# Raw feed-forward weights in eight tiles of two chunks instead of four of four

## Chip, core and metric

The kernel runs on one core of one Trainium2 chip. The metric is the device time of one execution in microseconds (us); lower is better. TensorE is called PE in the profile, VectorE DVE, ScalarE ACT, GpSimd POOL and the queue of SyncE SP.

## The reference, cut to what matters

A decoder layer on 256 tokens of width 2048: a SwiGLU feed-forward, a mixer (sliding-window attention beside RWKV-7), cross-attention into a memory, and a second SwiGLU feed-forward. The change touches the two feed-forwards.

```python
D_MODEL, D_FF, SEQ = 2048, 5632, 256

def swiglu(h, w_gate, w_up, w_down):
    return (jax.nn.silu(h @ w_gate) * (h @ w_up)) @ w_down

x = x + 0.5 * swiglu(rms_norm(x, ffn1_norm[l]), ffn1_w_gate[l], ffn1_w_up[l], ffn1_w_down[l])
x = gated_parallel_mixer(x, ...)
x = memory_cross_attention(x, mem, ...)
x = x + 0.5 * swiglu(rms_norm(x, ffn2_norm[l]), ffn2_w_gate[l], ffn2_w_up[l], ffn2_w_down[l])
return rms_norm(x, final_norm)
```

All weights are float32 and are read once: 46 MB for each of the six feed-forward matrices.

## The kernel before

**Precision.** Each product is made of three matmuls in a rounded 32-bit format (fp32r): a value is split into a rounded part "hi" and a remainder "lo", and hi*hi, lo*hi and hi*lo are added (`times`, lines 485 to 487). ScalarE casts "hi" (line 409) and VectorE subtracts "lo" (line 410), both in `split_unit`. The buffers "hi" and "lo" are rings of three units.

**Units and items.** A *unit* is two chunks (KU = 2) of 128 rows by 512 columns of one weight matrix, 512 KB. An *item* is what one step of the product loop uses: one unit, or, where two column blocks are worked on together, a unit of each. Such pairs are gate with up, and two column blocks of down. The text calls the first of a pair gate and the second up. `weight_plan` lists all products; `units` and `items` are made from it once, in the order of use.

**Seven products in place of eight.** Of an item of a pair, 2 x 2 blocks are multiplied, and some items (SEVEN: pairs 0, 2, 3 and 4 of the eight in a gate/up block; others in down) do it in seven products (21 matmuls) in place of eight (24). For these POOL adds a chunk of the gate unit into the first chunk of the up unit while transferring it from DRAM (line 366, an accumulating DMA, table `added`). Then VectorE makes three sums (lines 438, 439, 440 in `divide`), and these are split into "thi" and "tlo" (lines 417, 418). In the second feed-forward pair 3 is *staged*: its sums are made during the mixer, kept in DRAM and loaded (`staged`, `first_sums`, `load_sums`).

**Where raw weights lie.** In the feed-forwards raw weights are loaded by SP into tiles "raw2" of four chunks (1 MB), of which there are four. One such tile holds two units of the same matrix: those of an even pair and of the odd pair behind it. So the units stand in the order gate (even), gate (odd), up (even), up (odd), and the two items are (0, 2) and (1, 3) of these. In the mixer and at the first units of the second feed-forward the tiles "raw" hold one unit each.

**What orders the work.** `next_item` asks for the loads of the eight units from the current item on, then divides the current item and the ones after it (AHEAD = 2 units). SP's queue is in order, and a load waits until its tile's last reader is done, mostly a "lo". VectorE's and ScalarE's queues are in order too, but their order isn't the written one: a scheduler places each instruction at build time, by when it believes its inputs to be there. `product_pair` multiplies; after each group of products `bg.tick()` lets background steps (transposes, norms, sums of the activations) put in their instructions. A gate/up *block* is 512 columns of gate and up over all 16 chunks, eight items; three groups of four, four and three blocks are each followed by their down products. The text calls blocks of a group first, middle and last.

Of the kernel before, what the change touches and what calls it, by code (L numbers as in the profile page):

```python
# [7 lines left out]
F32 = mybir.dt.float32  # L8
F32R = mybir.dt.float32r
AF = mybir.ActivationFunctionType  # L10
ALU = mybir.AluOpType
# [4 lines left out]
P = 128  # L16
# [11 lines left out]
KU = 2  # L28
# [6 lines left out]
AHEAD, LOADED = 2, 4  # L35
# [4 lines left out]
SEVEN_2, STAGED = (0, 2, 3, 4), (3,)  # L40
# [60 lines left out]
def weight_plan(a):  # L101

    w = {n: v[0] for n, v in a.items() if "_w_" in n or n.startswith("w_")}
    yield from feed_forward_plan(w["ffn1_w_gate"], w["ffn1_w_up"], w["ffn1_w_down"], False)
    yield None
    w_in = w["w_in"]
    cols = [0, 512, ATTN_W]
    for c in cols:  # L110
        yield w_in, 0, KD, c, 512
    yield w_in, 0, KD, C_RW + 3 * RW, 288
    for h in range(2):
        yield w_in, 0, KD, C_RW + RW + h * 512, 512
    for n in range(4):
        yield w_in, 0, KD, C_GATE + n * 512, 512
        yield w["w_proj_attn"], 0, 8, n * 512, 512
    for h in range(2):
        yield w_in, 0, KD, C_RW + h * 512, 512
        yield w_in, 0, KD, C_RW + 2 * RW + h * 512, 512  # L120
    for n in range(4):
        yield w_in, 0, KD, C_GATE + D + n * 512, 512
    for n in range(4):
        yield w["w_proj_rwkv"], 0, 8, n * 512, 512
    for n in range(4):
        yield w["w_out"], 0, KD, n * 512, 512
    yield w["w_cross_kv"], 0, KD, 0, 512
    yield w["w_cross_q"], 0, KD, 0, 512
    yield w["w_cross_kv"], 0, KD, 512, 512
    for n in range(4):  # L130
        yield w["w_cross_o"], 0, 4, n * 512, 512
    yield None
    yield from feed_forward_plan(w["ffn2_w_gate"], w["ffn2_w_up"], w["ffn2_w_down"], True)
# [3 lines left out]
def decoder_layer(ctx: ExitStack, tc: tile.TileContext, a: dict, out: bass.AP):  # L137
    nc = tc.nc
    act, dve, pool, pe = nc.scalar, nc.vector, nc.gpsimd, nc.tensor
# [126 lines left out]
    def flat(x):  # L266
        x = x[0]
        return x if len(x.shape) == 1 else x.rearrange("h d -> (h d)")
# [6 lines left out]
    first = fill()  # L275
# [5 lines left out]
    v = flat(a["rwkv_mu"])  # L281
# [7 lines left out]
    def late_vectors():  # L289
        while "pow" not in at:  # L290
            yield
        with tc.issue_after(at["pow"].ins):
            pool.dma_start(sinks[:], a["attn_sinks"].broadcast_to([P, 16]))
            fetch_gains()
            fetch_rv()
        yield from idle(12)
        fill_gains()
        fill_rv()
        dve.tensor_scalar(nk_k[:], k_k, -1.0, None, ALU.mult)
        dve.tensor_scalar(ok_a[:], k_a, -1.0, 1.0, ALU.mult, ALU.add)  # L300
# [11 lines left out]
    plan, units, items, ends, staged = [], [], [], [], {}  # L312
    for entry in weight_plan(a):
        if entry is None:
            ends.append(len(units))
            continue
        plan.append(entry)
        w, k0, nk, c0, n = entry
        if not isinstance(w, tuple):
            for k in range(k0, k0 + nk, KU):  # L320
                items.append(((len(units),), False))
                units.append((w, k, c0, n))
            continue
        for k in range(k0, k0 + nk, 2 * KU):
            u = len(units)
            units += [(v, k + i, c, 512) for v, c in zip(w, c0) for i in (0, KU)]
            for i in range(2):
                q = (k - k0) // KU + i
                if len(ends) == 2 and n == SEVEN_2 and q in STAGED:
                    staged[len(items)] = len(staged)  # L330
                items.append(((u + i, u + 2 + i), q in n))
    raws, parts, summed = {}, {}, {}
    first_sums = {items[i][0][1]: n for i, n in staged.items()}
    added = {which[1]: which[0] for i, (which, seven) in enumerate(items) if seven and i not in staged}
    sums_d = dram.tile([len(staged), P, 4, 512], F32, name="sums")
    at = {"item": 0, "product": 0, "pool": None}

    def load(u, pieces=None):

        if u >= len(units) or u in raws:  # L340
            return
        w, k, c0, n = units[u]
        wide = at["pool"] is not None and (u < ends[0] or u >= ends[1] + LOADED)
        m = 2 if wide else 1
        if wide:
            raw = at["pool"].tile([P, m * KU, n], F32, tag="raw2", name="raw2", bufs=4)
        else:
            raw = wp.tile([P, KU, n], F32, tag="raw", name="raw", bufs=4)
        for i in range(m):
            raws[u + i] = raw[:, i * KU : (i + 1) * KU, :]  # L350
        first = [v for v in (u, u + 1)[:m] if v in first_sums]
        for v in first:
            nc.sync.dma_start(raws[v][:, 0], sums_d[first_sums[v], :, 0, :])
        if first:
            pieces = ((slice(1, 4), nc.sync),)
            if first[0] > u:
                pieces = ((slice(0, 2), nc.sync), (slice(3, 4), nc.sync))
            elif len(first) == 2:
                pieces = ((slice(1, 2), nc.sync), (slice(3, 4), nc.sync))
        for i, queue in pieces or ((slice(0, m * KU), nc.sync),):  # L360
            rows = slice((k + i.start) * P, (k + i.stop) * P)
            queue.dma_start(raw[:, i], w[rows, c0 : c0 + n].rearrange("(a p) n -> p a n", p=P))
        for v in (u, u + 1)[:m]:
            if v in added:
                w, k, c0, n = units[added[v]]
                pool.dma_start(  # L366
                    raws[v][:, 0], w[k * P : k * P + P, c0 : c0 + n], accum_op=ALU.add,
                )

    def load_sums(i):  # L370

# [72 lines left out]
    def next_item():  # L444
        i = at["item"]
        at["item"] += 1
        u = items[i][0][0]
        for v in range(u, u + (2 * LOADED if at["pool"] is not None else LOADED)):
            load(v)
        divide(i)  # L450
        room = AHEAD
        for j in range(i + 1, min(i + 1 + AHEAD, len(items))):
            room -= len(items[j][0])
            if room < 0:
                break
            for v in items[j][0]:
                load(v)
            load_sums(j)
            divide(j)
        load_sums(i + 2)  # L460
        return parts[i]
# [337 lines left out]
    def blk(d, n):  # L799
        return d[:, n * 512 : (n + 1) * 512].rearrange("(t p) n -> p t n", p=P)  # L800

    W = {n: v[0] for n, v in a.items()}
# [7 lines left out]
    def aligned(sp):  # L810

        return sp.tile([P, 16], F32, name="shift")


    with tc.tile_pool(name="f1", bufs=1, reuse_waits="tile") as sp:
        aligned(sp)
        at["pool"] = sp
        x = sp.tile([P, 2, D], F32, name="x")

        def col(n):  # L820
            return x[:, :, n * 512 : (n + 1) * 512]

        n1 = Norm(g_ffn1)
        nc.sync.dma_start(col(0), blk(W["x"], 0))
        load(0, ((slice(0, 1), act), (slice(1, 2), nc.sync), (slice(2, 4), nc.sync)))
        nc.sync.dma_start(col(1), blk(W["x"], 1))
        load(2, ((slice(0, 2), nc.sync), (slice(2, 4), nc.sync)))
        for n in range(2, 4):
            nc.sync.dma_start(col(n), blk(W["x"], n))
            load(2 * n)  # L830
        for n in range(4):
            bg.spawn("feat", n1.block(n, col(n)))
        bg.spawn("const", late_vectors())
        hold = {}

        def done1(n):
            if n == 0:
                hold["n"] = Norm(g_mix)
            pool.dma_start(blk(x1d, n), col(n))
            bg.spawn("feat", hold["n"].block(n, col(n)))  # L840

        feed_forward(sp, x, n1, W["ffn1_w_gate"], W["ffn1_w_up"], W["ffn1_w_down"], done1)
        n2 = hold["n"]
        bg.drain()
        at["pool"] = None


    with tc.tile_pool(name="mx", bufs=1, reuse_waits="tile") as sp:
# [3 lines left out]
        def t4(name, shape=(P, 4, T), dt=F32):  # L852
            return sp.tile(list(shape), dt, tag="t4", name=name, bufs=N4)
# [651 lines left out]
        for n in range(4):  # L1505
            g, m = t4("gl", (P, 2, 512)), t4("ml", (P, 2, 512))
# [102 lines left out]
    with tc.tile_pool(name="f2", bufs=1, reuse_waits="tile") as sp:  # L1609
        room = aligned(sp)  # L1610
        at["pool"] = sp
        x = sp.tile([P, 2, D], F32, name="x")
# [92 lines left out]
```

## Time and profile before

| | before |
|---|---|
| median of 3 runs | 2391.59 us (2387.91 to 2400.15) |
| the profiled execution | 2391.23 us, span 2389.5 us |
| mean granted TensorE clock | 0.983 |
| PE busy | 2278.7 us (95%) |
| DVE busy | 1810.1 us (76%) |
| ACT busy | 1260.0 us (53%) |
| POOL busy | 213.7 us (9%) |
| moved by DMA | 487 MB, 204 GB/s on the mean |

Busy times are of one profiled execution. The span runs from its first to its last instruction. Idle time of an engine counts only where another engine waits for it; who waited for whom is read from semaphore events. A DMA's time is that from its issue to its landing, and the mean share is that of the 16 DMA engines.

### The profile page before, as it was taken

Reading aid. Unit: us, or ns where it says so; the run is one execution under the profiler, and the core shown is the slowest. Engines: PE = TensorE matmul, PEld = TensorE weight load, DVE = VectorE, ACT = ScalarE, POOL = GpSimd, SP = SyncE. Lnnn points to the kernel's source line nnn. Section 1 sums busy time; section 2 is a strip of 40 time slices with the busy share of each in tenths; the row PEclk is TensorE's granted clock in tenths of the full one; section 3 lists DMA queues with packets and bytes.
Section 4 is the critical chain, followed back from the end, with each engine's and each line's share of the span. In section 5 each row is a group of like instructions: output and inputs, shape, how many; then the busy total and the mean of one; then the engine's idle time right before and its main releaser. Section 6 shows DMA issues by size and latency. Waiting matters only on the chain.

```text
span 2389.5 us, 28663 instructions
## 1 busy us (share of the span) xinstructions
PE 2278.7 (95%) x10557; PEld 1839.0 (77%) x10557; DVE 1810.1 (76%) x2332; ACT 1260.0 (53%) x1649; POOL 213.7 (9%) x293
## 2 busy tenths in 40 slices
PE   9999998999999999999999999999999989998998
PEld 7677776777777877788888887887778767776776
DVE  6897787987888667877556666567788778877886
ACT  6465454554555557534444546465555455544554
POOL 1000000000000101110321030000000000000000
PEclk9999999999999999999999999999999999999999
DMA  7666666666666645676768685557666766666664
GB/s 253 189 212 193 192 206 188 205 201 192 209 200 195 187 128 151 194 229 208 213 217 266 205 283 184 184 192 248 211 203 208 222 194 221 203 189 207 208 220 146
DMA packets 244973, 487.04 MB, mean 204 GB/s; under 512 B 17163, under 2 KB 19440, under 8 KB 244832
## 3 DMA queue, kind: packets, MB, share of 16 engines
q1 hardware_dynamic: 221952, 433.62, 54.6%
q0 software_dynamic: 22416, 50.79, 10.5%
q8 instruction: 83, 1.36, 0.2%
q10 hardware_dynamic: 464, 0.79, 0.1%
q14 instruction: 58, 0.48, 0.1%
HBM read 461.47 MB, written 23.59 MB: 203 GB/s over the span
## 4 chain that ended last, share of the span: by engine, by line
PE 48%; DMA 23%; DVE 22%; issue 5%; ACT 2%; SPq 0%; POOLq 0%; POOL 0%; DVEq 0%; ACTq 0%
PE acc L485 11%; PE acc L486 11%; PE acc L487 11%; DVE lo L410 10%; DMA raw<-in_ffn_w_gate_dram 10%; DMA raw<-in_ffn_w_up_dram 7%; DMA raw<-in_ffn_w_down_dram 5%; DVE tlo L418 3%; PE mm L486 2%; PE mm L487 2%; PE mm L485 2%; PE tr L676 2%; DVE raw L439 2%; DVE raw L440 1%; ACT hi L409 1%
## 5 line engine op out<-in xcount | busy, mean ns | idle before, releaser
L409 ACT CAST hi<-raw 128x1024 fp32r<-128x1024 f32 (+1 forms) x770 | 801.6, 1045 | 786.4 <-PE acc L487 478.8
L410 DVE TENSOR_TENSOR lo<-raw,hi 128x1024 fp32r<-128x1024 f32 (+1 forms) x770 | 930.7, 1214 | 331.7 <-ACT hi L409 330.2
L485 PE MATMUL acc<-hi,xhi 128*128 128x512 f32 (+1 forms) x1136 | 450.6, 399 | 2.7 <-ACT xhi L703 2.3
L486 PE MATMUL acc<-lo,xhi 128*128 128x512 f32 (+1 forms) x1136 | 445.1, 392 | 2.7 <-DVE lo L410 2.7
L487 PE MATMUL acc<-hi,xlo 128*128 128x512 f32 (+1 forms) x1136 | 442.8, 390 | 0.0
L485 PEld LDWEIGHTS acc<-hi,xhi 128*128 128x128 f32 x1136 | 215.4, 190 | 50.6 <-issue 4.0
L486 PEld LDWEIGHTS acc<-lo,xhi 128*128 128x128 f32 x1136 | 214.6, 189 | 50.4 <-DVE lo L410 8.0
L487 PEld LDWEIGHTS acc<-hi,xlo 128*128 128x128 f32 x1136 | 214.3, 189 | 44.6 <-DVE xlo L704 1.0
L417 ACT CAST thi<-raw 128x1024 fp32r<-128x1024 f32 x212 | 168.3, 833 | 131.2 <-DVE raw L439 126.2
L418 DVE TENSOR_TENSOR tlo<-raw,thi 128x1024 fp32r<-128x1024 f32 x212 | 196.0, 950 | 2.2 <-ACT thi L417 1.9
L438 DVE TENSOR_TENSOR raw<-raw 128x512 f32<-128x512 f32 x96 | 66.1, 689 | 153.3 <-DMA raw<-in_ffn_w_gate_dram 112.1
L486 PE MATMUL mm<-lo,xhi 128*128 128x512 f32 x360 | 144.1, 400 | 31.2 <-DVE lo L410 31.2
L487 PE MATMUL acc<-hi,hlo 128*128 128x512 f32 x372 | 146.3, 393 | 0.0
L485 PE MATMUL acc<-hi,hhi 128*128 128x512 f32 x372 | 146.1, 393 | 0.1
L486 PE MATMUL acc<-lo,hhi 128*128 128x512 f32 x372 | 146.1, 393 | 0.0
L487 PE MATMUL mm<-hi,xlo 128*128 128x512 f32 x360 | 142.1, 395 | 0.0
L485 PE MATMUL mm<-hi,xhi 128*128 128x512 f32 x360 | 141.5, 393 | 0.0
L366 POOL DMA_DIRECT2D raw<-in_ffn_w_gate_dram x70 | 60.4, 904 | 882.2 <-DMA raw<-in_ffn_w_up_dram 342.4
L486 PEld LDWEIGHTS mm<-lo,xhi 128*128 128x128 f32 x360 | 68.5, 190 | 50.0 <-DVE lo L410 36.6
L486 PE MATMUL mm<-lo,chi 128*128 128x512 f32 x200 | 80.5, 402 | 5.6 <-DVE lo L410 5.6
L485 PE MATMUL mm<-hi,chi 128*128 128x512 f32 x200 | 80.7, 413 | 3.4 <-DVE u L638 1.8
L485 PEld LDWEIGHTS acc<-hi,hhi 128*128 128x128 f32 x372 | 70.4, 189 | 15.9 <-DVE x L649 1.7
(399 smaller groups left out, 3723.6 us busy)
## 6 DMA issues: line engine op xcount, KB each, us to landing
raw<-in_ffn_w_down_dram SPq DMA_DIRECT2D x88, 1024.0 KB, 6.2
raw<-in_ffn_w_gate_dram SPq DMA_DIRECT2D x84, 1024.0 KB, 5.7
raw<-in_ffn_w_up_dram SPq DMA_DIRECT2D x78, 1024.0 KB, 7.0
raw<-in_w_in_dram SPq DMA_DIRECT2D x136, 512.0 KB, 3.8
raw<-in_ffn_w_gate_dram POOLq DMA_DIRECT2D x70, 256.0 KB, 4.3
raw<-in_w_out_dram SPq DMA_DIRECT2D x32, 512.0 KB, 4.5
raw<-in_w_proj_attn_dram SPq DMA_DIRECT2D x16, 512.0 KB, 4.0
raw<-in_w_proj_rwkv_dram SPq DMA_DIRECT2D x16, 512.0 KB, 4.7
```

Of the source, the lines that this page charges most:

```text
L366: pool.dma_start(raws[v][:, 0], w[k * P : k * P + P, c0 : c0 + n], accum_op=ALU.add,)
L409: at["hi"] = act.copy(hi[:, s], raw[:, s])
L410: at["lo"] = dve.tensor_tensor(lo[:, s], raw[:, s], f32(hi[:, s]), ALU.subtract)
L417: act.copy(hi[:], v[:, :n])
L418: dve.tensor_tensor(lo[:], v[:, :n], f32(hi[:]), ALU.subtract)
L438: dve.tensor_tensor(t[0][:, 0], ru[:, 1], ru[:, 0], ALU.add)
L439: dve.tensor_tensor(t[0][:, 1], t[0][:, 0], rg[:, 0], ALU.subtract)
L440: dve.tensor_tensor(t[1][:, 0], t[0][:, 0], rg[:, 1], ALU.add)
L485: pe.matmul(o, xh, hi, start=first, stop=False, **how)
L486: pe.matmul(o, xh, lo, start=False, stop=False, **how)
L487: pe.matmul(o, xl, hi, start=False, stop=last, **how)
L676: pe.transpose(b[:, o : o + P], tok[:, t, col : col + P], ident[:])
```

## The change

Units of a pair now stand in the order of their use (gate, up, gate, up), every item is two neighbouring units, and each unit has a tile "raw2" of its own: two chunks, 512 KB, eight tiles. The memory is the same. A tile is loaded by one transfer of 512 KB (two of 256 KB for the staged sums) where one of 1 MB was, and the special cases for two units in one tile are gone. At the start the loads of the first eight units are issued one by one, between the same loads of x. In the built program SP issues 850 transfers where it issued 600; POOL's 208 are the same. The instructions of the mixer stand in the same order on each engine; those of the feed-forwards on VectorE, ScalarE and TensorE are the same in number and kind, but the scheduler has put many of them in another order. Lines move up by 12 (line 438 is 426 after, 410 is 398, 366 is 354).

```diff
-        for k in range(k0, k0 + nk, 2 * KU):
-            u = len(units)
-            units += [(v, k + i, c, 512) for v, c in zip(w, c0) for i in (0, KU)]
-            for i in range(2):
-                q = (k - k0) // KU + i
-                if len(ends) == 2 and n == SEVEN_2 and q in STAGED:
-                    staged[len(items)] = len(staged)
-                items.append(((u + i, u + 2 + i), q in n))
+        for k in range(k0, k0 + nk, KU):
+            q = (k - k0) // KU
+            if len(ends) == 2 and n == SEVEN_2 and q in STAGED:
+                staged[len(items)] = len(staged)
+            items.append(((len(units), len(units) + 1), q in n))
+            units += [(v, k, c, 512) for v, c in zip(w, c0)]
...
         w, k, c0, n = units[u]
-        wide = at["pool"] is not None and (u < ends[0] or u >= ends[1] + LOADED)
-        m = 2 if wide else 1
-        if wide:
-            raw = at["pool"].tile([P, m * KU, n], F32, tag="raw2", name="raw2", bufs=4)
+        if at["pool"] is not None and (u < ends[0] or u >= ends[1] + LOADED):
+            raw = at["pool"].tile([P, KU, n], F32, tag="raw2", name="raw2", bufs=8)
         else:
             raw = wp.tile([P, KU, n], F32, tag="raw", name="raw", bufs=4)
-        for i in range(m):
-            raws[u + i] = raw[:, i * KU : (i + 1) * KU, :]
-        first = [v for v in (u, u + 1)[:m] if v in first_sums]
...
-        for i, queue in pieces or ((slice(0, m * KU), nc.sync),):
+        raws[u] = raw
+        if u in first_sums:
+            nc.sync.dma_start(raw[:, 0], sums_d[first_sums[u], :, 0, :])
+            pieces = ((slice(1, 2), nc.sync),)
+        for i, queue in pieces or ((slice(0, KU), nc.sync),):
             rows = slice((k + i.start) * P, (k + i.stop) * P)
             queue.dma_start(raw[:, i], w[rows, c0 : c0 + n].rearrange("(a p) n -> p a n", p=P))
-        for v in (u, u + 1)[:m]:
-            if v in added:
-                w, k, c0, n = units[added[v]]
-                pool.dma_start(
-                    raws[v][:, 0], w[k * P : k * P + P, c0 : c0 + n], accum_op=ALU.add,
-                )
+        if u in added:
+            w, k, c0, n = units[added[u]]
+            pool.dma_start(
+                raw[:, 0], w[k * P : k * P + P, c0 : c0 + n], accum_op=ALU.add,
+            )
...
         nc.sync.dma_start(col(0), blk(W["x"], 0))
-        load(0, ((slice(0, 1), act), (slice(1, 2), nc.sync), (slice(2, 4), nc.sync)))
-        nc.sync.dma_start(col(1), blk(W["x"], 1))
-        load(2, ((slice(0, 2), nc.sync), (slice(2, 4), nc.sync)))
-        for n in range(2, 4):
+        load(0, ((slice(0, 1), act), (slice(1, 2), nc.sync)))
+        load(1)
+        for n in range(1, 4):
             nc.sync.dma_start(col(n), blk(W["x"], n))
             load(2 * n)
+            load(2 * n + 1)
```

More of the change, by code (lines that the diff above doesn't have):

```diff
@@ L342, in load @@
         w, k, c0, n = units[u]
-        wide = at["pool"] is not None and (u < ends[0] or u >= ends[1] + LOADED)
-        m = 2 if wide else 1
-        if wide:
-            raw = at["pool"].tile([P, m * KU, n], F32, tag="raw2", name="raw2", bufs=4)
+        if at["pool"] is not None and (u < ends[0] or u >= ends[1] + LOADED):
+            raw = at["pool"].tile([P, KU, n], F32, tag="raw2", name="raw2", bufs=8)
         else:
             raw = wp.tile([P, KU, n], F32, tag="raw", name="raw", bufs=4)
-        for i in range(m):
-            raws[u + i] = raw[:, i * KU : (i + 1) * KU, :]
-        first = [v for v in (u, u + 1)[:m] if v in first_sums]
[L352 to L359, printed above, removed]
-        for i, queue in pieces or ((slice(0, m * KU), nc.sync),):
+        raws[u] = raw
[3 more added lines that the diff above has]
+        for i, queue in pieces or ((slice(0, KU), nc.sync),):
             rows = slice((k + i.start) * P, (k + i.stop) * P)
             queue.dma_start(raw[:, i], w[rows, c0 : c0 + n].rearrange("(a p) n -> p a n", p=P))
-        for v in (u, u + 1)[:m]:
-            if v in added:
-                w, k, c0, n = units[added[v]]
-                pool.dma_start(
-                    raws[v][:, 0], w[k * P : k * P + P, c0 : c0 + n], accum_op=ALU.add,
-                )
+        if u in added:
[3 more added lines that the diff above has]
+            )
     def load_sums(i):
```

## The prediction

> **What bounds the kernel now.** I read the busy time by stretches first, then the waits, then the timeline of one stall. The stretches are the first feed-forward (to about 760 us), the mixer and the second feed-forward (from about 1625 us); columns are us, then each engine's busy us (instructions), the granted clock, DMA share and GB/s.
>
> ```profile
> span 2389.5 us, 28663 instructions
> 60.00:760.00 700.00, 655.35 (x2807) 521.14 (x2807) 587.13 (x723) 362.76 (x413) 46.57 (x54) 0.98 0.65 198
> 760.00:1625.00 865.00, 856.75 (x4461) 703.34 (x4459) 569.32 (x779) 461.32 (x716) 118.35 (x167) 1.00 0.66 205
> 1680.00:2389.50 709.50, 660.27 (x2828) 528.81 (x2827) 572.09 (x702) 368.37 (x422) 36.52 (x45) 0.97 0.64 203
> ```
>
> TensorE is at work 99% of the mixer and 93 to 94% of the feed-forwards: 45 us and 49 us stand idle there, and the change touches the feed-forwards alone. VectorE is at 84% and 81% there, near enough to TensorE that a pause of VectorE is felt. DMA moves the same 200 GB/s at the same share in all three, so it isn't bytes that are short. What pauses VectorE shows in the waits (total us, times, longest):
>
> ```profile
> DVE raw L438 <- DMA raw<-in_ffn_w_gate_dram: 112.1, 45, 6.6
> ACT hi L409 <- DMA raw<-in_ffn_w_gate_dram: 67.1, 17, 6.7
> PEld mm L486 <- DVE lo L410: 56.9, 26, 5.7
> PE mm L486 <- DVE lo L410: 46.4, 20, 5.3
> DVE raw L438 <- DMA raw<-in_ffn_w_down_dram: 41.1, 18, 5.6
> SPq L362 <- DVE lo L410: 562.0, 110, 14.1
> ```
>
> Line 438 is the first sum of a seven-product item. It reads the up tile after POOL's accumulating transfer (line 366) has added a gate chunk to it. VectorE stood 153 us before these sums (112.1 + 41.1, 63 of 96 times), and TensorE's largest waits are for the "lo" that stand behind them. The last row (asked for the first 760 us alone) is SP's: its loads wait for VectorE's "lo", since that releases a raw tile. So there is a loop: release, load, accumulation, sum, next release. One worst turn of it, on the timeline:
>
> ```profile
> 343.73 2.35 DVE L410 TENSOR_TENSOR lo<-raw,hi 128x1024 fp32r<-128x1024 f32 x2
> 345.00 0.37 SPq L362 DMA_DIRECT2D raw<-in_ffn_w_gate_dram  x1
> 346.10 0.37 SPq L362 DMA_DIRECT2D raw<-in_ffn_w_up_dram  x1
> ...
> 352.42 1.21 DVE L410 TENSOR_TENSOR lo<-raw,hi 128x1024 fp32r<-128x1024 f32 x1
> 353.55 0.68 DVE L439 TENSOR_TENSOR raw<-raw,raw 128x512 f32<-128x512 f32 x1
> 354.16 0.68 DVE L440 TENSOR_TENSOR raw<-raw,raw 128x512 f32<-128x512 f32 x1
> 354.76 1.21 DVE L410 TENSOR_TENSOR lo<-raw,hi 128x1024 fp32r<-128x1024 f32 x1
> 355.75 0.86 POOL L366 DMA_DIRECT2D raw<-in_ffn_w_gate_dram  x1 [12.86 <-DMA raw<-in_ffn_w_up_dram]
> 363.40 0.69 DVE L438 TENSOR_TENSOR raw<-raw 128x512 f32<-128x512 f32 x1 [5.70 <-DMA raw<-in_ffn_w_gate_dram]
> 365.29 0.80 PE L486 MATMUL mm<-lo,xhi 128*128 128x512 f32 x1 [5.25 <-DVE lo L410]
> ```
>
> The second "lo" of the first row ends at 346.1 and frees the tile. Gate's and up's megabyte are issued 1.1 us apart at 346, up has landed at 355.7, the accumulation at 363.4: 17.3 us from release to sum. VectorE pauses 5.70 us, TensorE 5.25: nearly one for one. The rows also give VectorE's steps: 1.13 us from one 128x1024 operation to the next, 0.60 for 128x512.
>
> Four gate/up blocks without a down product (columns as before), and the waits before their sums:
>
> ```profile
> 293.80:480.40 186.60, 172.34 (x735) 136.97 (x735) 156.99 (x193) 98.79 (x113) 13.04 (x15) 0.97 0.66 199
> 340.70:391.00 50.30, 44.66 (x187) 35.51 (x186) 39.94 (x48) 25.55 (x30) 3.47 (x4) 0.93 0.64 188
> L438 DVE TENSOR_TENSOR raw<-raw 128x512 f32<-128x512 f32 x15 | 10.3, 688 | 16.6 <-DMA raw<-in_ffn_w_gate_dram 16.5
> 349.21 0.39 PE L485 MATMUL mm<-hi,xhi 128*128 128x512 f32 x1
> 349.43 0.39 PE L486 MATMUL mm<-lo,xhi 128*128 128x512 f32 x1
> 349.66 0.40 PE L487 MATMUL mm<-hi,xlo 128*128 128x512 f32 x1
> ```
>
> Matmuls start 0.227 us apart when nothing waits. A block has 4 x 21 + 4 x 24 = 180 of them (seven-product and plain items), so 40.8 us, with its transposes about 41.4; four take 166 of the 186.6 us. The 21 us lost stand against 16.6 us of waiting before sums: again about one for one, and a little over. The block with the 5 us stall has a granted clock of 0.93, so 3.5 of its 50.3 us went at a reduced clock behind the stall. [...]
>
> **What the change does to this loop.** In the feed-forwards each load becomes two of half the size. Their transfers, by KB and median us from issue to landing:
>
> ```profile
> raw<-in_ffn_w_gate_dram SPq DMA_DIRECT2D x84, 1024.0 KB, 5.7
> raw<-in_ffn_w_up_dram SPq DMA_DIRECT2D x78, 1024.0 KB, 7.0
> raw<-in_ffn_w_gate_dram POOLq DMA_DIRECT2D x70, 256.0 KB, 4.3
> raw<-in_ffn_w_up_dram SPq DMA_DIRECT2D x10, 512.0 KB, 4.6
> raw<-in_w_cross_q_dram SPq DMA_DIRECT2D x8, 512.0 KB, 3.6
> DMA to landing us min/median/max: 4.0/4.3/8.2
> ```
>
> (The last row is that of line 366, POOL's accumulations.) *Response*, from the "lo" that frees an up tile to the sum that reads the next one in it: now 7.0 + 4.3 + 0.1 for two hand-offs = 11.4 by medians, 17.3 at worst. Afterwards a half tile: 4.6 + 4.3 + 0.1 = 9.0. Bounds: 3.6 + 4.0 = 7.6 below, 7.0 + 8.2 = 15.2 above (as if neither were quicker for the smaller load). I take 9.0, nearest to the row that is up's own half-size load beside the same accumulations; 8 to 10 seems likely, as half as many bytes are queued around an accumulation.
>
> *Cover*, what lies between that release and that sum. A half tile is freed by its own item and no longer by the later of two, so in the program as written a sum is four items behind its release where the first of a pair was three. But VectorE's queue isn't in written order: the build moves each sum up to where it believes the data to be there, and the changed program has other places. For each of the 96 sums I took from the built programs VectorE's operations between (at 1.13 and 0.60 us) and the matmuls between those that free the "hi" buffers of the "lo" around them (at 0.227), the larger counts. Example, changed program, pair 0 of one block to pair 2 of the same:
>
> ```
> lo(up, pair 6 before)   frees the tile; its hi waits for matmul 1297
> tlo 1024, tlo 512, lo(gate, pair 7), lo(up, pair 7)   the last one's hi waits for matmul 1321
> sum(pair 2)   waits for the accumulation
> lo(gate, pair 0) ...
> ```
>
> VectorE's work is 1.13 + 0.60 + 2 x 1.13 = 4.0 us, the matmuls 24 x 0.227 = 5.4: cover 5.4, where the same sum in the old program has 10.9. Over all sums the old covers are 7.5 to 12.3 but for ten longer; the new ones are 5.4 to 5.7 (18 sums: mainly pair 2 of the middle blocks, and the first sum behind a down product), 6.8 (11: pair 0 of these blocks), 7.5 to 8.3 (10), and 9.9 to 17.1 (57). So the change shortens the response by 2.4 us or more, lengthens the cover of most sums and shortens that of the first three groups.
>
> *Sum.* At a response of 9.0, VectorE's waits are 18 x 3.5 + 11 x 2.2 + 10 x 1.0 = 97 us, against 153 now. At 8 the same table gives 59, at 10 it gives 136, and at 10.3 it gives 153. So 56 us less waiting at 9.0. I credit four fifths: today's waits reach TensorE one for one, but the removed ones are followed by waits of another kind ("thi", and "hi" for TensorE), which then come last. That is 45 us.
>
> A check on a middle block, from its own loop: from sum(pair 2) to the "lo" that ends pair 4 VectorE has 13 operations of 1.13, 15 of 0.60 and 2 of 0.66, 25.0 us; then a response; then three sums, one "hlo" and a "lo", 3.7 us; then a response. 28.7 + 2 x 9.0 = 46.7 us, against 186.6 / 4 = 46.65 today. Middle blocks gain nothing, then; the gain is in the downs, the first and the last blocks of each group.
>
> **The rest of the diff.** 250 more load issues on SP at 0.37 us are 93 us on a queue that waited 562 us for VectorE in the first 760: hidden between releases 1.13 us apart or more; if not, an issue delays the next by 0.37, which is inside the spread of the response. VectorE gets 205 more semaphore waits:
>
> ```profile
> L438 DVEq EVENT_SEMAPHORE  x86: 21/21/21, 47.8 to 2328.9; - x86
> ```
>
> At 0.02 us these are 4 us at most, run ahead in the queue: nothing to 4. A load's semaphore lane is that of the eighth load before, which then is the load whose tile it takes: no wait beyond the tile's. At the start the same bytes come in the same order. Staged pair 3 of the second feed-forward has the same transfers. The mixer's instructions stand in the same order. All nothing.
>
> So 2391.2 - 45 = 2346 us for the profiled execution (span 2389.5 and 1.7 around it), which is within 0.4 us of the median of the runs shown; the forecast for the median is the same.
>
> **Rivals.**
> Slower: responses don't shrink as the rows of idle queues suggest, for loads are now issued at every "lo" and the accumulation always has company (its landing went to 8.2 us today where two megabytes were issued beside it). The early sums then cost more than the old ones. It decides at 10.3 us; at 11 the table gives 188 us of waiting, 35 more than now: 2426 us. For it: 29 covers are under 7 us. Against it: half the bytes in flight per issue. Chance 0.14.
>
> Slower by size: half-size transfers use the engines worse. If each held the queue for its 3.6 us, a pair of 7.2 us would stand against 5.2 us of matmuls per item, and the feed-forwards' 1520 us would grow by 7.2/5.2, to some 2970 us in all. The mixer speaks against it: it runs on half-size loads at 205 GB/s for a share of 0.66, as the feed-forwards do on whole ones. [...] Chance 0.02.
>
> No change: the middle blocks turn worse by what the others gain, or VectorE's own work (587 of 700 us) sets the end: 2391 us. Chance 0.14.
>
> Faster still: early sums wait where TensorE has two or three units (5 to 8 us of matmuls) queued, so most of the 97 us never reaches it: 110 us gained, 2280 us. Against it, the loop of the middle block, which no queue ahead shortens. Chance 0.08.
>
> **How the numbers follow.** The forecast (response 8 to 10) has 0.62. Its own range is the table's: at 8, four fifths of 94 gives 2316; at 10, of 17, gives 2378. The range goes on to 2400, the response of 10.5 at which the slower rival begins to tell; beyond it lie most of the slower rivals and of the faster one, 0.2 together. About 0.5% (12 us) is what a measurement of this kernel can tell from no change: faster 0.62 + 0.08 = 0.70, same 0.14, slower 0.16.
>
> **What would show it.** In the profile after: half-size loads of up landing in 4 to 5 us, accumulations near 4.3 to 5; line 438's waits (line 426 there) down from 153 to about 97 us and shared by fewer sums; none to speak of in the down products and the last blocks, 2 and 3.5 us before pairs 0 and 2 in middle blocks; those blocks still 46 to 47 us long; the mixer unchanged. I am wrong if up's half load and accumulation take over 10.3 us together, if the waits fall and TensorE's idle time doesn't, or if middle blocks shrink to 42 us.

## The result, and the profile after

The changed kernel took 2405.53 us in the median of 20 runs (2399.58 to 2417.26), the kernel before, on the same chip and beside it, 2395.05 us (2376.14 to 2424.58). The ratio is 1.0049 with a 95% interval of 1.0028 to 1.0071: slower by half a per cent, where 2346 us was forecast. The time is 5.5 us beyond the range and the change went the other way. The difference of 10.5 us lies inside the 12 us that the prediction took as no change; over 20 runs of each it is clear all the same. The profiled execution took 2410.43 us, its span is 2408.7 us, its mean granted clock 0.972 (0.983 before).

The stretches of the changed kernel, columns as in the prediction; the last two are a middle and a last block of the first feed-forward:

```profile
60.00:760.00 700.00, 653.30 (x2790) 526.37 (x2789) 582.77 (x717) 367.00 (x408) 46.20 (x53) 0.96 0.68 198
760.00:1640.00 880.00, 876.98 (x4553) 720.64 (x4552) 587.48 (x812) 475.14 (x735) 117.61 (x167) 1.00 0.64 207
1690.00:2408.70 718.70, 654.96 (x2759) 526.04 (x2757) 561.53 (x687) 364.38 (x412) 36.13 (x44) 0.95 0.64 194
342.10:392.10 50.00, 44.44 (x190) 35.33 (x189) 40.26 (x49) 25.84 (x29) 3.50 (x4) 0.97 0.67 189
433.90:475.80 41.90, 41.90 (x189) 34.15 (x188) 38.86 (x49) 24.92 (x29) 2.62 (x3) 1.00 0.75 220
```

The mixer stands as it did. TensorE is idle for 47 us of the first feed-forward (45 before) and for 64 us of the second (49 before), and both have a lower clock. A last block runs without a gap, a middle block takes 50.0 us. Line 426 (the first sum) with the idle time of VectorE ahead of it, then the rows of the transfers, then line 354 (POOL's accumulations) with who waited for them:

```profile
L426 DVE TENSOR_TENSOR raw<-raw 128x512 f32<-128x512 f32 x96 | 66.1, 689 | 203.8 <-DMA raw<-in_ffn_w_gate_dram 137.1 <-DMA raw<-in_ffn_w_down_dram 38.9 <-issue 26.9
raw<-in_ffn_w_up_dram SPq DMA_DIRECT2D x166, 512.0 KB, 4.6
raw<-in_ffn_w_gate_dram POOLq DMA_DIRECT2D x70, 256.0 KB, 5.7
raw<-in_ffn_w_down_dram POOLq DMA_DIRECT2D x26, 256.0 KB, 5.9
  DVE raw L426: 176.0, 39
DMA to landing us min/median/max: 3.9/5.7/7.9
```

VectorE waited 204 us before these sums where it had waited 153. (The 27 us put down to "issue" are waits for accumulations too: eight of these nine sums start 0.08 us after the landing, the ninth 0.43 us.) The load of up is quicker, as forecast, 4.6 us. The accumulation is slower: 5.7 us in the median where it took 4.3, and 5.74 us on the mean where it took 5.02. One turn of the loop shows why (start, us, engine, line; idle before it in brackets):

```profile
363.68 1.22 DVE L398 TENSOR_TENSOR lo<-raw,hi 128x1024 fp32r<-128x1024 f32 x1
364.92 0.37 SPq L351 DMA_DIRECT2D raw<-in_ffn_w_up_dram  x1
...
366.66 0.37 SPq L351 DMA_DIRECT2D raw<-in_ffn_w_gate_dram  x1
...
369.17 0.88 POOL L354 DMA_DIRECT2D raw<-in_ffn_w_gate_dram  x1 [19.88 <-DMA raw<-in_ffn_w_up_dram]
369.36 0.37 SPq L351 DMA_DIRECT2D raw<-in_ffn_w_up_dram  x1
...
371.23 0.37 SPq L351 DMA_DIRECT2D raw<-in_ffn_w_gate_dram  x1
375.95 0.69 DVE L426 TENSOR_TENSOR raw<-raw 128x512 f32<-128x512 f32 x1 [4.76 <-DMA raw<-in_ffn_w_gate_dram]
```

The first "lo" frees the tile at 364.9 and the load is issued at once; the accumulation goes out at 369.2 and has landed at 375.9: 6.8 us, with two loads issued into it at 369.4 and 371.2. Release to sum is 11.0 us, not 9.0. Before, loads came in bursts of megabytes; now every "lo" releases one, and the pauses between bursts are gone. For each of the 96 accumulations I added up from the trace the KB of SP's loads that lay in flight beside it (of each load the share of its time that overlaps). Before: 641 KB on the mean, and 59 accumulations of 4.0 to 4.6 us with 325 KB. After: 942 KB; 12 accumulations under 4.6 us with 533 KB, 45 between 5.5 and 6.5 us with 988, and 20 above that with 1214.

### The profile page after: what moved, and what is told of

Read it like the earlier page. It is cut to its first block, busy times and chain, and to the rows that moved or that the text cites. A ratio compares the mean times of both kernels' runs of the same rounds, so it can differ in the third digit from the quotient of the medians.

```text
span 2408.7 us, 29377 instructions
## 1 busy us (share of the span) xinstructions
PE 2289.9 (95%) x10557; PEld 1857.7 (77%) x10557; DVE 1813.3 (75%) x2332; ACT 1271.5 (53%) x1649; POOL 213.9 (9%) x293
## 4 chain that ended last, share of the span: by engine, by line
PE 61%; DMA 16%; DVE 15%; issue 6%; ACT 1%; POOLq 0%; SPq 0%; DVEq 0%; POOL 0%; ACTq 0%
PE acc L473 13%; PE acc L474 13%; PE acc L475 13%; DMA raw<-in_ffn_w_gate_dram 9%; DVE lo L398 7%; DMA raw<-in_ffn_w_up_dram 4%; PE mm L473 4%; PE mm L474 4%; PE mm L475 4%; DMA raw<-in_ffn_w_down_dram 3%; DVE tlo L406 2%; PE tr L664 2%; PE mm L1348 1%; PE tr L474 1%; DVE raw L427 1%
## 5 line engine op out<-in xcount | busy, mean ns | idle before, releaser
L405 ACT CAST thi<-raw 128x1024 fp32r<-128x1024 f32 x212 | 173.7, 835 | 141.8 <-DVE raw L427 71.0
L473 PE MATMUL mm<-hi,hhi 128*128 128x512 f32 x176 | 73.3, 417 | 30.7 <-DVE u L647 30.7
L474 PEld LDWEIGHTS acc<-lo,hhi 128*128 128x128 f32 x372 | 72.0, 194 | 27.6 <-DVE lo L398 13.1
```

What stands on the lines that cost most here:

```text
L405: act.copy(hi[:], v[:, :n])
L473: pe.matmul(o, xh, hi, start=first, stop=False, **how)
L474: pe.matmul(o, xh, lo, start=False, stop=False, **how)
```

## The experiments

Two questions were open: is it the accumulation's company (the loads in flight beside it) that lost the gain, and what is the loop worth without its wait? Each ratio is to the kernel before, run beside it. "Waits" is the idle time of VectorE ahead of the first sums; "loss" is the time over the quickest kernel here (2244.9 us).

| kernel | accumulation, load of up (median us) | waits us | median us | ratio to before, 95% | loss |
|---|---|---|---|---|---|
| before | 4.3, 7.0 | 153 | 2395 | | 150 |
| after | 5.7, 4.6 | 204 | 2405.5 | 1.0049 [1.0028, 1.0071] | 161 |
| e5_light | 4.8, 3.9 | 137 | 2339.3 | 0.975 [0.971, 0.979] | 94 |
| e1_held | 5.9, 5.0 | 0 | 2252.5 | 0.940 [0.935, 0.944] | 8 |
| e1b | 5.8, 4.8 | 9 | 2244.9 | 0.937 [0.932, 0.941] | 0 |
| e1c | 5.8, 5.0 | 54 | 2261.8 | 0.943 [0.938, 0.949] | 17 |
| e2_before_held | 4.4, 7.2 | 127 | 2382.0 | 0.993 [0.990, 0.997] | 137 |
| e3_old_order | 5.8, 4.2 | 226 | 2430.4 | 1.014 [1.008, 1.021] | 185 |
| e3h | 5.8, 4.6 | 1 | 2251.9 | 0.940 [0.934, 0.946] | 7 |
| e4_split | 4.2, 5.6 | 144 | 2356.5 | 0.986 [0.978, 0.993] | 112 |
| e4h | 4.3, 6.5 | 46 | 2285.1 | 0.954 [0.948, 0.960] | 40 |

**The cover alone.** Three kernels are the changed one with the first sum held back: an edge for the scheduler puts it behind a "lo" of an item before. Both are VectorE's, so nothing is added but the place in its queue. Held behind the newest "lo" (e1_held), behind the one before that (e1b), and behind the one before that (e1c), the shortest covers worked out as in the prediction are 15.0, 12.2 and 9.5 us in place of 5.4.

```diff
             t = [wp.tile([P, KU, 512], F32, tag="raw", name="raw", bufs=4) for _ in range(2)]
-            dve.tensor_tensor(t[0][:, 0], ru[:, 1], ru[:, 0], ALU.add)
+            with tc.issue_after(at["lo"].ins):
+                dve.tensor_tensor(t[0][:, 0], ru[:, 1], ru[:, 0], ALU.add)
```

In e1b the edge is to `at["lo1"]`, in e1c to `at["lo2"]`, which `split_unit` keeps ahead of each "lo":

```diff
+            at["lo2"], at["lo1"] = at.get("lo1"), at.get("lo")
```

> The changed kernel with one edge more: the first sum of an item is queued on VectorE behind the last lo of the item before, as written, so that its cover is 15 us or more where it was 5.4 to 6.8 for 29 sums. Theory (early sums meet a response of 10.5 to 11 us): the waits before the sums fall from 204 us to under 20, TensorE's loss in the feed-forwards by two thirds, and the time to 2290 to 2340 us. Rival 1 (half-size transfers use the engines worse): the response is what it is, loads stay late, 2395 us or more. Rival 2 (VectorE's own work sets the end, waits only change their names): waits fall, the time stays within 12 us of 2405.

> As the one before, but each first sum is held one lo less far back: covers of 12.2 us and more. Theory: waits before sums under 25 us, the time within 10 us of the run with covers of 15. Rivals as there.

> As the two before, held two lo less: covers of 9.5 us and more, 36 of them under 11. Theory: at a response of 10.5 to 11 the waits are 11 to 30 us, the time within 20 us of the run with covers of 15 and not under it by more than 10. If the response is longer than I read it, here it shows: at 13 the waits would be 110 us.

Measured: 2252.5, 2244.9 and 2261.8 us. The first is 38 us below its range. The waits of e1c, 54 us, are more than the 11 to 30 expected: the response is longer than the 10.5 to 11 us assumed, 11.2 on the mean in its trace (from the issue of the load to the landing of the accumulation). The accumulations are as slow as in the changed kernel, and so are the loads; the sum comes later and doesn't find them missing. Both rivals are out: the waits went and the time with them. One feed-forward and the first sum's row of e1_held, then the sum's row of e1b:

```profile
60.00:760.00 700.00, 699.62 (x3127) 571.88 (x3126) 632.39 (x779) 405.40 (x476) 52.70 (x78) 1.00 0.74 218
L427 DVE TENSOR_TENSOR raw<-raw 128x512 f32<-128x512 f32 x96 | 65.7, 684 | 0.1
```

```profile
L428 DVE TENSOR_TENSOR raw<-raw 128x512 f32<-128x512 f32 x96 | 65.7, 685 | 8.7 <-DMA raw<-in_ffn_w_down_dram 6.9 <-DMA raw<-in_ffn_w_gate_dram 1.9
```

TensorE is at work in 699.6 of 700 us. The whole loss hung on the place of this one instruction, and with it went more than was expected. The best of them, e1b, takes 6.3% less than the kernel before and 6.7% less than the changed one.

**The same edge on the kernel before** (the same two lines in its `divide`).

> The kernel before with the same edge as the first run: covers of 10.2 to 11.6 us for most sums, where they were 7.5 to 12.3. Theory: a pair's tile is still freed late and its megabytes are late together (response 11.4 to 17), so waits stay at 100 to 150 us and the time at 2360 to 2400 us. Rival 2: no change. If place in the queue were all and the size of the tiles nothing, this would reach the same time as the first run.

```profile
DVE raw L439 <- DMA raw<-in_ffn_w_gate_dram: 84.5, 33, 6.8
DVE raw L439 <- DMA raw<-in_ffn_w_down_dram: 42.2, 16, 5.8
```

Its waits are 127 us and its time is 2382.0: with 1 MB tiles in pairs the edge brings covers of 10.2 to 11.6 us only for the shortest third, as a tile is freed by the later of its two items. The edge is worth 13 us here and over 150 in the changed kernel. The half-size tiles come with half-size transfers; which of the two makes the difference is taken apart below.

**Order of use, or size?** The changed kernel with the units in the old order (gate, gate, up, up), without the edge (e3_old_order) and with it (e3h):

```diff
-        for k in range(k0, k0 + nk, KU):
-            q = (k - k0) // KU
-            ...
-            items.append(((len(units), len(units) + 1), q in n))
-            units += [(v, k, c, 512) for v, c in zip(w, c0)]
+        for k in range(k0, k0 + nk, 2 * KU):
+            u = len(units)
+            units += [(v, k + i, c, 512) for v, c in zip(w, c0) for i in (0, KU)]
+            for i in range(2):
+                q = (k - k0) // KU + i
+                ...
+                items.append(((u + i, u + 2 + i), q in n))
```

> Half-size tiles in the old order, sums where the build puts them: 4.8 to 7.6 us of cover for 37 sums. Theory: at a response of 10.5 to 11 us the waits are 170 to 200 us and the time is 2385 to 2420 us, like the changed kernel's. Rival (the order of use does harm): under 2360.

> Half-size tiles and transfers as in the changed kernel, but units in the old order (gate even, gate odd, up even, up odd), and sums held behind the last lo of the item before: covers of 12.9 us and more. It tells the size of the tiles from the order of the loads. Theory: at a response near 11 us the waits before sums are under 20 us and the time is 2245 to 2270 us, as with the order of use. Rival (the order of use is what pays once sums are held): 2300 us or more.

Unheld it took 2430.4 us, 10 more than the upper end expected, with 226 us of waits where 170 to 200 were; held, 2251.9 us and 1 us of waits. The order of use is worth some 25 us as long as sums come early, which its longer covers would give, and nothing once they are held. So what counts of the change is the size, of the tiles or of the transfers.

**Tile size, or transfer size?** The kernel before with its 1 MB tiles, each filled by two transfers of 512 KB, without the edge (e4_split) and with it (e4h):

```diff
-        for i, queue in pieces or ((slice(0, m * KU), nc.sync),):
+        for i, queue in pieces or [(slice(j, j + KU), nc.sync) for j in range(0, m * KU, KU)]:
```

> The kernel before with each megabyte loaded by two transfers of 512 KB, sums where the build puts them: 20 sums with covers of 5.2 to 7.5 us. Theory: at a response of 11 to 12 us waits are 166 to 241 us, so 2395 to 2450 us; smaller transfers let the build put sums earlier and nothing else gets quicker. Rival (small transfers land earlier, and that pays): under 2380.

> The kernel before (four tiles of four chunks, old order) with each megabyte loaded by two transfers of 512 KB, and sums held: covers of 10.2 to 11.6 us for most sums. It has the small transfers without the small tiles. Theory: tiles are still freed in pairs, the response is 11.5 to 13 us, waits are 30 to 150 us, the time is 2340 to 2390 us. Rival (the size of the transfer is what counts, for good): near 2250; (for ill): clearly over the 2382 of the same kernel with whole transfers.

Both were misses: 2356.5 and 2285.1 us, each far under what was expected. I had looked for the accumulation to suffer as it does in the changed kernel, and it doesn't. The sum's row, the transfers and who waited for the accumulations in e4_split:

```profile
L438 DVE TENSOR_TENSOR raw<-raw 128x512 f32<-128x512 f32 x96 | 66.1, 689 | 144.5 <-DMA raw<-in_ffn_w_gate_dram 109.6 <-DMA raw<-in_ffn_w_down_dram 34.6
raw<-in_ffn_w_up_dram SPq DMA_DIRECT2D x166, 512.0 KB, 5.6
raw<-in_ffn_w_gate_dram POOLq DMA_DIRECT2D x70, 256.0 KB, 4.2
  ACT hi L409: 14.1, 3
```

The loads are as small as in the changed kernel and as many, yet the accumulation takes 4.2 us: they still come in bursts (the tile is freed as a whole), with 450 KB beside an accumulation. So small transfers as such didn't slow it here; loads spread over all the time did (942 KB beside an accumulation and 5.7 us in the changed kernel). A unit no longer has to wait for its neighbour's half megabyte, nor has ScalarE: in the kernel before its casts waited for these accumulations as well:

```profile
  DVE raw L438: 153.2, 63
  ACT hi L409: 64.8, 15
```

The waits before the sums fell by 9 us only and the time by 39; the 51 us less of ScalarE's waits fit the rest, but nothing here takes these alone away.

Together with the runs above this tells the two sizes apart, all in the old order. Held, the kernel with 1 MB tiles goes from 2382.0 to 2285.1 us by small transfers (97 us), and by small tiles on top of them to 2251.9 (e3h, 33 us). Unheld, small transfers bring 39 us, and small tiles on top of them cost 74 (2356.5 to 2430.4). So most of the gain with held sums is the transfers', and the tiles pay only once the sums are held.

In this loop two transfers of 512 KB to a tile (e4_split) beat one of 1 MB (the kernel before): 0.986 of the time (0.978 to 0.993).

**The company itself.** The changed kernel, with a quarter of the pairs' bytes left out and all else in place. Its built program gives the same 96 covers as the changed kernel's.

```diff
+    firsts = {which[0] for which, _ in items if len(which) == 2}
...
-        raws[u] = raw
+        half = u in firsts and tuple(raw.shape) == (P, KU, 512) and not pieces
+        raws[u] = raw[:, 0:1, :].to_broadcast([P, KU, n]) if half else raw
+        if half:
+            pieces = ((slice(0, 1), nc.sync),)
```

> The changed kernel, but of the first unit of every pair (gate, and the first column block of a pair of down) only one of its two chunks is loaded, 256 KB in place of 512, and the product uses it twice. That leaves out a quarter of the bytes of the pairs and nothing on the engines; the places of the sums, and so the covers worked out from the built program, are the same (5.4 to 5.7 for 18, 6.8 for 11, 7.5 to 8.3 for 10). Theory (an accumulation is slow by the load bytes beside it): beside an accumulation lie some 700 KB on the mean where the changed kernel has 942, the median accumulation falls from 5.7 to between 4.5 and 5.2 us, the response to about 9, the waits before the sums from 204 to between 100 and 150 us, and the time to between 2330 and 2385 us. Rival (the accumulation is slow for another reason, such as that it adds into a tile which has only just landed, or the small size of the tile): accumulations stay at 5.5 to 5.9 us, the waits at 185 to 210 us, and the time at 2390 to 2415 us.

```profile
L430 DVE TENSOR_TENSOR raw<-raw 128x512 f32<-128x512 f32 x96 | 65.9, 687 | 136.8 <-DMA raw<-in_ffn_w_gate_dram 97.6 <-DMA raw<-in_ffn_w_down_dram 25.5 <-issue 11.5
raw<-in_ffn_w_up_dram SPq DMA_DIRECT2D x166, 512.0 KB, 3.9
raw<-in_ffn_w_gate_dram POOLq DMA_DIRECT2D x70, 256.0 KB, 4.8
```

Beside an accumulation lie 635 KB, where some 700 were expected; the rest is within what the theory gave: 4.9 us for it (median of all 96), 137 us of waits, 2339.3 us. From the changed kernel to this one the waits fall by 67 us and the time by 66. Not all of it is the accumulation's: the load of up became quicker as well, 3.9 us for 4.6. Of the 1.4 us by which the mean response fell, 0.8 are the accumulation's. The rival, a slowness of the accumulation's own, is out. The same dependence holds from kernel to kernel, by the mean accumulation and the mean KB beside it: 4.61 us at 450 (e4_split), 4.94 at 635 (e5_light), 5.02 at 641 (before), 5.74 at 942 (after), 5.93 at 1109 (e1_held), about 0.2 us for each 100 KB; the others lie within 0.3 us of that line. A longer transfer has more beside it for that reason alone, so the slope is a rough one: counted over the first 3.9 us of every accumulation, the same five have 329, 506, 427, 660 and 711 KB, which gives about 0.34 us for each 100 KB and leaves before and e5_light out of order by 0.1 us.

## Why the prediction was wrong, by its steps

**Load of up, 4.6 us: right**, to the tenth.

**Accumulation, 4.3 us: mis-sized, and the step that failed.** It measured 5.7 (gate) and 5.9 (down). The reason given for keeping 4.3, "as half as many bytes are queued around an accumulation", is wrong: half as many are queued per issue, but at every "lo", and the bytes beside an accumulation rose from 641 to 942 KB. So the response by medians is 4.6 + 5.7 + 0.1 = 10.4 where the forecast had 9.0, past the 10.3 from which, by the prediction, the slower rival decides. This rival, to which it gave 0.14, named the mechanism that e5_light shows.

**Two hand-offs, 0.1 us: mis-sized as well.** From the landing of the up load to the start of POOL's transfer pass 0.56 us (median of the 96 in the kernel before and the changed one alike); the other hand-offs take 0.02 us each. This is half a microsecond in every response, before and after.

**The comparison 97 against 153: wrong on its own.** 97 us is the table's, from median durations; 153 is the trace's. On the old program the same table, at its own 7.0 + 4.3 + 0.1 = 11.4, gives 81 us. Like against like it was 81 before and 97 after: no gain, with no accumulation slowed at all. The median accumulation hides the late ones (4.3 us, but 5.02 on the mean), and 0.5 us of hand-off is missing. It takes 0.9 us more in the response (12.3) for the table to give the old kernel's waits (148). With these 0.9 us added to each kernel's own medians, the table can be held against all of them:

| kernel | response + 0.9 | table | measured waits |
|---|---|---|---|
| after | 11.3 | 208 | 204 |
| e5_light | 9.7 | 124 | 137 |
| e3_old_order | 11.0 | 198 | 226 |
| e4_split | 10.8 | 153 | 144 |
| e2_before_held | 12.6 | 109 | 127 |
| e4h | 11.8 | 50 | 46 |
| e1c | 11.8 | 59 | 54 |
| e1b | 11.6 | 0 | 9 |

The covers and the table hold to within some 30 us, then, with one number fitted to the kernel before; what went into them was wrong. With 0.9 added and the accumulation left at 4.3 the table gives 132 for the changed kernel, at 5.7 it gives 208: the response from medians and too short a hand-off was worth 35 us of waiting, the accumulation 76.

The traces give the same without a fit. For each of the 96 sums the load of its up tile was found as the last one landed before the accumulation. On the mean, load, hand-off and accumulation are 6.4 + 0.6 + 5.0 = 12.1 us before and 4.4 + 0.6 + 5.7 = 10.7 after: the change did shorten the response, by 1.4 us where 2.4 was forecast. But VectorE came to 31 of the sums within 8 us of the load's issue, and to 9 before. With each sum left where it is and each response of the changed kernel cut by 0.7 us (the accumulation's growth on the mean), its waits come to 167 us; cut by 1.4 us (its growth in the median), to 134. By this estimate most of the waits come from the early places, the slower accumulation added 35 to 70 us, and without it the waits would have stayed near the 153 of before.

**Four fifths of the waits: right in size, but not the whole of the time.** The changed kernel's 204 us of waits cost 161 us, near four fifths; the 153 us before cost 150. So 51 us more of waiting brought 10 us, not 41. What was left out of the sum is ScalarE's row, "ACT hi L409" waiting for the gate transfer, 67.1 us, which stands among the prediction's quoted rows and isn't used in it. In the changed kernel 3.8 us of these waits are left, and none of them is for an accumulation (line 426 is its only waiter). That they make up the difference fits e4_split as well, but wasn't tried by itself.

How the waits reach TensorE changed too. The prediction looked for waits of another kind behind "thi" and "hi"; they came behind "u", VectorE's sums of finished products. TensorE's waits, the first row from before, the others from after, and one case of the third row:

```profile
PE mm L485 <- DVE u L638: 1.8, 5, 0.5
PE mm L474 <- DVE lo L398: 42.9, 23, 3.1
PE mm L473 <- DVE u L647: 30.7, 8, 4.4
PE mm L473 <- DVE u L626: 17.6, 10, 2.2
```

```profile
230.80 0.68 DVE L646 TENSOR_TENSOR u<-tr,u 128x512 f32<-128x512 f32 x1
237.17 0.69 DVE L426 TENSOR_TENSOR raw<-raw 128x512 f32<-128x512 f32 x1 [5.69 <-DMA raw<-in_ffn_w_down_dram]
237.78 0.68 DVE L647 TENSOR_TENSOR u<-mm,u 128x512 f32<-128x512 f32 x1
238.52 0.80 PE L473 MATMUL mm<-hi,hhi 128*128 128x512 f32 x1 [3.92 <-DVE u L647]
```

The early sum stood in VectorE's queue ahead of line 647, which reads a finished product in "mm"; TensorE's next matmul into "mm" waited for that. So a sum placed too early held up what stood behind it, not its own item alone. All eight waits for line 647 (31 us), and 9 of the 18 us for line 626, stand behind a sum that waited.

**The clock: under-weighed.** The prediction's sum has no term for it. Busy TensorE for the same 10557 matmuls, before, after and in e1b:

```profile
PE 2278.7 (95%) x10557; PEld 1839.0 (77%) x10557; DVE 1810.1 (76%) x2332; ACT 1260.0 (53%) x1649; POOL 213.7 (9%) x293
```

```profile
PE 2289.9 (95%) x10557; PEld 1857.7 (77%) x10557; DVE 1813.3 (75%) x2332; ACT 1271.5 (53%) x1649; POOL 213.9 (9%) x293
```

```profile
PE 2225.9 (99%) x10557; PEld 1826.8 (81%) x10557; DVE 1813.5 (81%) x2332; ACT 1266.9 (56%) x1649; POOL 213.5 (10%) x293
```

Of the 163 us that the span of the changed kernel is longer than e1b's (2245.3), 64 are busy time. Counting in the trace stretches of at least four matmuls that start at half the pace (0.40 to 0.50 us apart, not 0.227): 16 before, which cost 25 us, 24 after, 43 us, and one in e1b, 1 us. These account for some 40 of the 64 us; the rest stays open. TensorE's longest pause became shorter, 4.4 us where it was 5.3, but its pauses of 2 us and more rose from 18 to 23, and the clock's loss with them: 11 of the 19 us between the spans of before and after are busy time. In the block with a clock of 0.93 the prediction took 3.5 us for the time at a reduced clock. They are what the block lost: the clock's record has 6.8 us at half.

**The blocks: right in kind.** The last block shown has no stall (41.9 us with TensorE busy throughout); the middle block shown has two waits, of 4.8 and 4.7 us, in place of 2 and 3.5. It takes 50.0 us, not 46 to 47, for both responses are longer: 28.7 + 2 x 11 is 50.7 by the prediction's own loop. The down products were to be nearly free of waits and aren't: 38.9 us of line 426's idle time ended with an accumulation from the down weights.

**SP's 250 issues and the 205 semaphore waits, at nothing: right**, as far as the runs show: e4_split issues as many and is faster, and e1b has both and TensorE is never short. **The mixer, unchanged: right** (877.0 of 880 us busy). **Rivals of size:** no sign of half-size loads using the engines worse; e1_held moves 218 GB/s in the stretch where the kernel before moved 198.

## What to carry to other kernels

Run a model of waits on the kernel whose trace is at hand before it is used on the changed one, and compare model with model: here that would have turned the sign. Splitting tiles and transfers shortened the release-to-use loop here (12.1 to 10.7 us on the mean), but paid in full only with the consumer placed late enough as well: where a scheduler places it by its own idea of when data lands, one ordering edge can be worth more (6% here) than the whole change of tiling. A steadier stream of loads took away the quiet gaps in which small transfers ran (641 to 942 KB beside an accumulation, 4.3 to 5.7 us for it in the median), so the time of such a transfer has to be taken at the bytes that will lie beside it.

## What the hardware showed that I had not expected

A 256 KB accumulating transfer took 4.0 to 4.6 us with some 300 KB of loads beside it (59 of 96 in the kernel before) and over 6.5 us with 1.2 MB (20 of 96 in the changed one), about 0.2 us more for each 100 KB over the kernels. TensorE fell to half its pace behind short pauses: of the 24 slow stretches in the changed kernel 11 within the feed-forwards had no single pause over 2.5 us in the 7 us before them; all their pauses together were 1.9 to 4.4 us.

The record of the granted clock shows more. In the traces of the kernel before and the changed one all its changes lie on a grid of 3.41 us. In these two TensorE ran at the full clock through 1338 of these steps. Behind 43 of them the clock was halved, and in these TensorE stood idle, by the profile's busy time, for 49 to 100% of the step; behind the other 1295 it wasn't, and none of them was idle for more than 56%. A halved clock came back behind steps that were idle for at most 13%, and stayed halved behind those of 17% and more. So in these two traces pauses within one step added up, and about half a step was enough. The nine other kernels keep to this but for one step of e1b, halved at 37%, and one of e5_light, back at 16.5%.
